# One pass over the in-projection's weights and one over the second half-step's, for all 576 tokens of a decoder step

## The chip, the cores and the metric

The kernel runs on one core of a Trainium2 chip. The metric is the device time of one execution in microseconds (us). In the profile PE is the matrix engine, DVE the vector engine, ACT the scalar engine, POOL the general engine and SP the engine that here only issues transfers. Each engine works through its own instructions in their order, and semaphores between them make one wait for another.

## The reference

One inference step of a two-layer decoder: 512 prompt tokens and 64 sample tokens (8 sequences of 8), 1024 features. Layer 0 is a half-step (SwiGLU), attention, a half-step; layer 1 is a half-step, a state space layer, a half-step. A layer norm stands behind each of the six.

```python
def ffn_residual(x, w_gate, w_up, w_down, g, b):
    return layer_norm(DN_ALPHA * x + FFN_RES * swiglu(x, w_gate, w_up, w_down), g, b)
for l in range(DEPTH):
    yp = ffn_residual(yp, ffn_w_gate[l, 0], ...); ys = ffn_residual(ys, ...)
    if l % 2 == 0:
        mp, ... = attn_mixer_prompt(yp, attn_w_in[i], attn_sinks[i], attn_w_out[i])
        ms, ... = attn_mixer_sample(ys, cache_a_k[i], cache_a_v[i], cache_b_k[i], cache_b_v[i], ...)
    else:
        ...  # state space layer
    yp = layer_norm(DN_ALPHA * yp + mp, ...); ys = layer_norm(DN_ALPHA * ys + ms, ...)
    yp = ffn_residual(yp, ffn_w_gate[l, 1], ...); ys = ffn_residual(ys, ...)
```

The attention has two mixers: A (8 heads, a mixture of three dilated windows over up to 2048 positions) and B (8 query heads over 2 key heads, the last 128 positions, with learned sinks). Prompt tokens attend within the prompt; sample tokens attend to 2048 cached keys and values per sequence and to their own.

## The kernel before, in words

Features lie on partitions, tokens are columns: `r` holds the residual, `xh` and `xl` the input of the next product as a pair (high and low part, float32r), so each product of a 128x128 block of weights is three matmuls (`product`). Columns come in two groups: GA (256, prompt) and GB (320: 64 sample tokens and 256 prompt tokens). `Weights` streams weights in units of at most 8 such blocks: SP loads a unit into a raw buffer (4 of them), ACT makes the high part (`hi`, L138), DVE the low part (`lo`, L145), into one of a few slots.

The order of the work is the order in which Python emits it. `hook()` runs after each product: it takes a step of what stands in `bg` (layer norms), else a step of each of the two tracks `lo[0]` and `lo[1]`, whose generators hold the attention in small steps. `lo_drain` steps the tracks until both are empty, with no product between.

- **Half-steps.** `ffn_joint` (layer 0, first) takes both groups per unit. `ffn_fast` (both of layer 1) does so too, and computes pairs of chunks of gate and up in seven block products instead of eight (`pair_run`). The second half-step of layer 0 is neither: `ffn_group` takes one group alone, so its weights are streamed twice, once for GA and once for GB, and there are no pairs.
- **In-projection.** Nine pairs of units, tiles of up to 128 tokens; a job (`in_job`) is 24 matmuls of 256 columns, `in_post` rotates queries and keys (`rope`: DVE, then POOL L1213) and later turns them (L1220). Group GA's 18 jobs come first, then 27 of GB with the weights streamed again.
- **Prompt attention.** 32 tasks, one for a pair of heads (A) or two heads (B) and a tile of 128 queries `p` = 0..3: scores (L1312), add bias and take the least value (DVE L1314), exponential (ACT L1321), scale (DVE L1325), three steps later transposes (L1337) and a copy (ACT L919), two steps later the product with the values (L1358, L1381) and `put_o` into `xh`, `xl`. The 16 tasks of p = 0, 1 run beside GB's projection, those of p = 2, 3 beside GA's half-step.
- **Samples.** `far_keys`: 48 steps, each of which issues the load of the next 128x512 tile `kc` of cached keys (ACT's queue, one ahead), multiplies a tile by the queries (DVE L1416) and adds it up (DVE L1417). `sample_b` is mixer B. `near` does one sequence's last 512 keys and values (2 MB each in two loads, 8 sequences); `far_values` streams 24 tiles `vc` of 512 KB (L1643). `near` starts only when `far_keys` is done (`first`).
- **Out-projection.** `end_group` for GA after the first 16 tasks, for GB (`out_b_now`) after all else of the attention, before the last part of GA's half-step; then follow the rest of GA's half-step and all of GB's (`ffn_b`).

So the emission order around the change is: 42 in-projection jobs; out-projection GA; 3 jobs; half-step GA without its last product, beside prompt attention, far keys and mixer B; near keys and far values in `lo_drain`; out-projection GB; end of half-step GA; half-step GB; layer 1.

## Time and profile before

| what | before |
|---|---|
| runs | 2422.57, 2427.65, 2423.44 us, median 2423.44 |
| profiled execution | span 2425.8 us from first to last instruction; its own time is not listed apart from the three runs |
| PE busy | 2313.1 us, 95% of the span |
| DVE, ACT, POOL busy | 1574.4, 946.3, 249.5 us |
| DMA | 307.04 MB, mean 127 GB/s |

Busy times say how long an engine had work in it, not how fast the work went. The granted clock (PEclk) is that of PE in tenths of full speed: 1.0 is 2.4 GHz, 0.5 is 1.2 GHz.

### The profile page before, as it was taken

The page shows a single profiled execution, that of the slowest core. Times are in us where ns is not written, and L with a number is a line of the kernel's source. Part 1 is how long each engine was busy: PE and PEld are TensorE (multiplying, and loading weights), DVE is VectorE, ACT ScalarE, POOL GpSimd, SP SyncE. Part 2 cuts the span into 40 slices and gives each one's busy share as a digit, 9 for nine tenths or more (in the row PEclk, how much of TensorE's full clock was granted, in tenths as well). Part 3 has the DMA queues.
Part 4 walks back from the last instruction along what each step waited for, and adds up shares of the span by engine and source line. Part 5 has one row for each costly group of instructions (what it writes and reads, how often), then busy time and mean ns, then how long its engine had stood idle before and what let it go on. Part 6 is the DMA issues. An engine that isn't in the chain of part 4 may idle for free.

```text
span 2425.8 us, 43680 instructions
## 1 busy us (share of the span) xinstructions
PE 2313.1 (95%) x17751; PEld 2241.5 (92%) x17751; DVE 1574.4 (65%) x3185; ACT 946.3 (39%) x1683; POOL 249.5 (10%) x388
## 2 busy tenths in 40 slices
PE   8999999999989988589999999999999999999998
PEld 8999999998878886379999999999999999999997
DVE  5878776766887765157544657667755565585675
ACT  3222232345476535135433433324346534342342
POOL 2012112131111000101100100000133101000000
PEclk9999999999999999689999999999999999999999
DMA  6244445354744798535655223423245312233241
GB/s 163 81 127 122 133 126 155 115 153 129 170 121 132 209 246 253 212 127 157 174 149 147 61 79 88 114 65 110 75 166 181 92 56 80 72 88 105 70 122 40
DMA packets 450858, 307.04 MB, mean 127 GB/s; under 512 B 13960, under 2 KB 420704, under 8 KB 450656
## 3 DMA queue, kind: packets, MB, share of 16 engines
q1 hardware_dynamic: 434944, 268.65, 38.0%
q0 software_dynamic: 7808, 20.38, 3.1%
q10 hardware_dynamic: 7904, 15.21, 2.2%
q8 instruction: 140, 2.29, 0.4%
q14 instruction: 62, 0.51, 0.1%
HBM read 282.07 MB, written 22.12 MB: 125 GB/s over the span
## 4 chain that ended last, share of the span: by engine, by line
PE 54%; DVE 8%; DMA 6%; ACT 4%; issue 2%; POOL 0%; SPq 0%; ACTq 0%; DVEq 0%; POOLq 0%
PE mm L588 11%; PE mm L587 11%; PE mm L589 11%; PE mm L736 4%; PE mm L738 4%; PE mm L737 4%; DMA kc<-in_cache_a_k_dram 2%; PE mm L580 2%; DMA vc<-in_cache_a_v_dram 2%; PE mm L582 2%; PE mm L584 2%; DVE wl L145 2%; ACT s L1321 1%; DMA wraw<-in_ffn_w_gate_dram 1%; DVE kc L1416 1%
## 5 line engine op out<-in xcount | busy, mean ns | idle before, releaser
L587 PE MATMUL mm<-xh,wh 128*128 128x320 f32 (+1 forms) x1880 | 562.8, 299 | 2.1 <-ACT xh L1664 1.2
L589 PE MATMUL mm<-xh,wl 128*128 128x320 f32 (+1 forms) x1880 | 558.9, 297 | 3.7 <-DVE wl L145 3.7
L588 PE MATMUL mm<-xl,wh 128*128 128x320 f32 (+1 forms) x1880 | 559.2, 297 | 0.1
L138 ACT CAST wh<-wraw 128x1024 fp32r<-128x1024 f32 (+2 forms) x440 | 437.0, 1001 | 303.0 <-PE mm L588 186.3
L145 DVE TENSOR_TENSOR wl<-wraw,wh 128x1024 fp32r<-128x1024 f32 (+2 forms) x440 | 508.2, 1165 | 39.7 <-ACT wh L138 39.4
L587 PE MATMUL mm<-hh,wh 128*128 128x320 f32 (+1 forms) x1408 | 421.7, 300 | 2.2 <-ACT hh L677 1.5
L589 PE MATMUL mm<-hh,wl 128*128 128x320 f32 (+1 forms) x1408 | 417.8, 297 | 5.2 <-DVE wl L145 5.2
L588 PE MATMUL mm<-hl,wh 128*128 128x320 f32 (+1 forms) x1408 | 417.4, 296 | 0.1
L589 PEld LDWEIGHTS mm<-xh,wl 128*128 128x128 f32 x1880 | 358.3, 191 | 4.9 <-DVE wl L145 4.9
L587 PEld LDWEIGHTS mm<-xh,wh 128*128 128x128 f32 x1880 | 358.6, 191 | 4.1 <-ACT xh L1664 1.6
L588 PEld LDWEIGHTS mm<-xl,wh 128*128 128x128 f32 x1880 | 358.5, 191 | 1.9 <-DVE xl L531 1.6
L589 PEld LDWEIGHTS mm<-hh,wl 128*128 128x128 f32 x1408 | 267.7, 190 | 6.0 <-DVE wl L145 6.0
L587 PEld LDWEIGHTS mm<-hh,wh 128*128 128x128 f32 x1408 | 267.8, 190 | 4.7 <-ACT hh L677 1.7
L588 PEld LDWEIGHTS mm<-hl,wh 128*128 128x128 f32 x1408 | 267.9, 190 | 0.8 <-DVE hl L679 0.3
L834 DVE TENSOR_TENSOR hf<-sg,mm 128x256 f32<-128x256 f32 (+1 forms) x128 | 57.8, 451 | 195.2 <-PE mm L589 96.3
L677 ACT CAST hh<-hf 128x256 fp32r<-128x256 f32 (+1 forms) x128 | 55.5, 433 | 307.4 <-DVE hf L834 307.4
L533 POOL TENSOR_SCALAR r<-r,lnb 128x256 f32<-128x256 f32 (+1 forms) x80 | 74.4, 947 | 867.3 <-DVE xl L531 867.3
L667 DVE TENSOR_TENSOR r<-r,mm 128x256 f32<-128x256 f32 (+1 forms) x96 | 43.3, 451 | 110.2 <-PE mm L589 110.2
L736 PE MATMUL mm<-sh,wh 128*128 128x288 f32 x384 | 113.5, 296 | 0.0
L737 PE MATMUL mm<-sl,wh 128*128 128x288 f32 x384 | 113.3, 295 | 0.0
L738 PE MATMUL mm<-sh,wl 128*128 128x288 f32 x384 | 113.0, 294 | 0.0
L1241 PE MATMUL mm<-wl,xh 128*128 128x256 f32 (+1 forms) x360 | 99.3, 288 | 8.8 <-DVE wl L145 8.8
(513 smaller groups left out, 4119.1 us busy)
## 6 DMA issues: line engine op xcount, KB each, us to landing
wraw<-in_ffn_w_gate_dram SPq DMA_DIRECT2D x110, 512.0 KB
wraw<-in_ffn_w_up_dram SPq DMA_DIRECT2D x110, 512.0 KB
wraw<-in_ffn_w_down_dram SPq DMA_DIRECT2D x80, 512.0 KB
wraw<-in_ffn_w_down_dram SPq DMA_DIRECT2D x40, 384.0 KB
wraw<-in_attn_w_in_dram SPq DMA_DIRECT2D x28, 512.0 KB
kc<-in_cache_a_k_dram ACTq DMA_DIRECT2D x48, 256.0 KB
vc<-in_cache_a_v_dram SPq DMA_DIRECT2D x24, 512.0 KB
kw<-in_cache_a_k_dram SPq DMA_DIRECT2D x16, 512.0 KB
```

The source lines that it names most:

```text
L138: self.nc.scalar.copy(u.h[:, :u.n], u.src)
L145: self.nc.vector.tensor_tensor(u.l[:, :u.n], u.src, u.h[:, :u.n].bitcast(F32), op=OP.subtract)
L533: nc.gpsimd.tensor_scalar(r[:, c, self.g], r[:, c, self.g], lnb[:, k:k + 1], self.scale, op0=OP.add, op1=OP.mult)
L587: nc.tensor.matmul(ps, u.h[:, ws(k)], th[:, k, g], start=k == 0, stop=False)
L588: nc.tensor.matmul(ps, u.h[:, ws(k)], tl[:, k, g], start=False, stop=False)
L589: nc.tensor.matmul(ps, u.l[:, ws(k)], th[:, k, g], start=False, stop=k == nk - 1)
L677: nc.scalar.copy(hh[:, c, t], hf)
L736: nc.tensor.matmul(ps, u.h[:, ws], xh_[:, k], start=k == 0, stop=False)
L737: nc.tensor.matmul(ps, u.h[:, ws], xl_[:, k], start=False, stop=False)
L738: nc.tensor.matmul(ps, u.l[:, ws], xh_[:, k], start=False, stop=k == 3)
L834: nc.vector.tensor_tensor(hf, sg, pu, op=OP.mult)
L1241: nc.tensor.matmul(ps, x, w, start=j == 0, stop=j == len(mms) - 1)
```

## The change

The in-projection takes all five tiles for each unit (the first three of nine pairs of units still in two sweeps, GA before GB, since GB's layer norm ends in between). All prompt attention and the far keys run beside the in-projection, and what is left of them in a `lo_drain` behind it. Since `xh`, `xl` are still the projection's input then, early outputs of the attention go to `r` (`put_o`), whose content is spilled to DRAM (`spill`, `fill`) and read back. Then come GA's out-projection with mixer B and the near keys on the tracks, a `lo_drain` for the rest of the samples, and GB's out-projection. The second half-step is one `ffn_fast` for both groups. The far keys' multiplications move from DVE to POOL, are loaded two ahead, and are added up one step later. `lo_drain` also pumps weights.

```diff
-P = {..., 'lr': 32, ...}
+P = {..., 'lr': 0, ...}
...
     def lo_drain():
         while any(t.busy() for t in lo):
             for t in lo:
                 t.step()
+            W.pump()
...
-            self.eps = eps4 if idx in (3, 5) else eps
-            self.scale = 1.0 if idx in (2, 4) else ALPHA
+            self.eps = eps4 if idx in (2, 3, 5) else eps
+            self.scale = 1.0 if idx in (1, 2, 4) else ALPHA
...
     def put_o(ps, c, t):
-        """a piece of the mixers' output, features on partitions, as the pair of the out projection"""
-        nc.scalar.copy(xh[:, c, t], ps)
-        nc.vector.tensor_tensor(xl[:, c, t], ps, xh[:, c, t].bitcast(F32), op=OP.subtract)
+        if o_waits[0]:
+            nc.scalar.copy(r[:, c, t], ps)
+            early_o.append((c, t))
+        else:
+            pair_o(ps, c, t)
...
-                    kc = kp.tile([128, 512], F32, name="kc")
+                    kc = kp.tile([128, 512], F32, name="kc", bufs=4)
                     q_far.dma_start(kc, far_rows(a["cache_a_k"], t, l, 1))
                     ks.append(kc)
+            def add_up(kc, l, t):
+                nc.vector.tensor_reduce(s_o[:, t, :, 0:2, l], kc.rearrange("p (j h d) -> p j h d", j=4, d=64), axis=AX.X, op=OP.add)
             load(0)
+            load(1)
             yield
+            last = None
             for i, (l, t) in enumerate(todo):
                 if t == 0:
                     q = qs.popleft()
-                load(i + 1)
+                load(i + 2)
                 kc = ks.popleft()
-                nc.vector.tensor_tensor(kc, kc, q, op=OP.mult)
-                nc.vector.tensor_reduce(s_o[:, t, :, 0:2, l], kc.rearrange("p (j h d) -> p j h d", j=4, d=64), axis=AX.X, op=OP.add)
+                nc.gpsimd.tensor_tensor(kc, kc, q, op=OP.mult)
+                if last:
+                    add_up(*last)
+                last = kc, l, t
                 yield
+            add_up(*last)
...
-        in_run(in_a, (0, 1), 2)
+        n0 = 3
+        jobs = [(ui, pair, i) for ui, pair in ins[:n0] for i in (0, 1)]
+        in_run(jobs, 2)
+        spill(GA)
         drain_bg()
-        lo[0].add([counted(g) for p in (0, 1) for g in prompt_tasks(prompt_a, p) + prompt_tasks(prompt_b, p)], P["pw"], P["pg"])
-        in_run(in_b[:P["fk"]], (2, 3, 4))
+        spill(GB_P)
+        o_waits[0] = True
+        W.slots(4)
+        in_run([(ui, pair, i) for ui, pair in ins[:n0] for i in (2, 3, 4)], 2)
         lo[1].add([far_keys()])
...
-        end_group(GA, out_a, xh, xl, NK, ev_add, 1, wait=P["wa"], spread=P["sa"])
-        in_run(in_b[P["nb"]:8], (2, 3, 4))
...
+        in_run(tile_jobs(n0, 4))
+        open_sm()
+        in_run(tile_jobs(4, 5))
+        lo[0].add(tasks(prompt_b, range(4)), P["pw"], P["pg"])
+        in_run(tile_jobs(5, 7))
+        lo[0].add(tasks(prompt_a, (0, 1)), P["pw"], P["pg"])
+        in_run(tile_jobs(7, 9))
+        in_flush()
+        o_waits[0] = False
+        lo[0].add(tasks(prompt_a, (2, 3)), P["pw"], P["pg"])
+        for g in (GA, GB_P):
+            for c in range(NK):
+                lo[1].add([from_r(c, g)], 2)
+            lo[1].add([fill(g)], 1, 1, True)
+        lo_drain()
...
+        mixer_b, near, far = sample_tasks(sa)
+        lo[1].add([mixer_b])
+        lo[0].add(near, P["sw"], P["sg"])
+        lo[0].add([far], 1, 1, True)
+        end_group(GA, out_a, xh, xl, NK, ev_add, 1, wait=P["wa"], spread=P["sa"])
+        drain_bg()
+        lo_drain()
+        st_s2.close()
+        st_s.close()
+        end_group(GB, out_b, xh, xl, NK, ev_add, 1, wait=1, spread=P["sb"])
...
-    attention(in_a, in_b, out_a, out_b, ffn_a)
+    attention(ins, out_a, out_b)
     W.slots(P["s8"])
-    ffn_group(ffn_b, GB, 2, wait=P["w0"])
+    ffn_fast(ffn01, 2, ahead=P["ah1"], wait=P["w1"], nslots=P["sn"], after=8)
     ffn_fast(ffn10, 3, ahead=P["ah1"], wait=P["w1"], nslots=P["sn"], after=4)
```

Three places show what moves. First, DVE beside GB's in-projection before the change: a far key step (L1416, L1417) stands between a rotation (L1202, L1207) and the next.

```order
L1149 TENSOR_TENSOR xl<-mm,xh 128x128
L1416 TENSOR_TENSOR kc<-kc,qb 128x512
L1417 TENSOR_REDUCE s_o<-kc 128x4x2
L1202 TENSOR_TENSOR sg<-mm,cos 128x256
L1207 TENSOR_TENSOR hf<-mm,sin 128x4x32 x2
```

In the changed kernel POOL has the multiplication (L1335), between the sum of a rotation (`rot`, L1123) and a copy of the sinks (L1285); DVE keeps the adding up (L1324 there). Behind the last rotation 24 multiplications follow each other on POOL, and then the reading back of `r` (L1602).

```order
L1123 TENSOR_TENSOR rot<-sg,hf 128x256
L1285 COPY s<-sink 128x2
L1335 TENSOR_TENSOR kc<-kc,qb 128x512
L1285 COPY s<-sink 128x2
L1335 TENSOR_TENSOR kc<-kc,qb 128x512 x24
L1602 DMA r<-d_r 128x8x256 x2
L1429 MEMSET blk_8509 128x128
```

So 48 multiplications leave DVE's row and stand in POOL's, 24 of them with nothing else around. Second, PE in the later half of the prompt attention, before: a product of GA's half-step (L580, L582, L584) stands between each task's pieces (values L1358, transposes L1337, scores L1312).

```order
L1312 MATMUL mm<-kT,qT_5547 128x512 x2
L580 MATMUL mm<-xh,wh_8490 128x256 x8
L582 MATMUL mm<-xh,wl_8491 128x256 x8
L584 MATMUL mm<-xl,wh_8490 128x256 x8
L1358 MATMUL mm<-pt,v 64x128 x6
L1337 MATMUL mm<-ident,s 128x128 x8
```

And in the changed kernel, behind the last job of the in-projection (values L1272, transposes L1251, scores L1226): twelve tasks more start behind it in this way, and no product is between them.

```order
L1272 MATMUL mm<-pt,v 64x128 x4
L1251 MATMUL mm<-ident,s 128x128 x6
L1226 MATMUL mm<-kT,qT_5564 128x128 x2
L1272 MATMUL mm<-pt,v 64x128 x6
L1251 MATMUL mm<-ident,s 128x128 x8
L1226 MATMUL mm<-kT,qT_5564 128x128 x2
```

Products have left this place. Third, PE where the near keys begin (transposes of `kw`). Before, they stand behind the last product of the half-step's part, and far key scores and the rest of the samples follow with no product.

```order
L589 MATMUL mm<-xh,wl_10945 128x256
L1526 MATMUL mm<-ident,kw 128x128 x16
L1517 MATMUL mm<-ident,s_o 128x128 x6
L1542 MATMUL mm<-kt,blk_9484 32x512 x4
L1545 MATMUL mm<-k_s,blk_9484 32x8 x4
L1526 MATMUL mm<-ident,kw 128x128 x16
```

In the changed kernel the first of them stands behind the first product of GA's out-projection, and the second product follows.

```order
L549 MATMUL mm<-xh,wh_7646 128x256
L550 MATMUL mm<-xl,wh_7646 128x256
L551 MATMUL mm<-xh,wl_7647 128x256
L1447 MATMUL mm<-ident,kw 128x128 x16
L549 MATMUL mm<-xh,wh_7649 128x256
L550 MATMUL mm<-xl,wh_7649 128x256
```

So seven of the eight products of GA's out-projection now stand among the first steps of the samples.

## Rows read from the trace of the kernel before

**Rows 1.** The page: busy times in us (share of the span), instructions.
```profile
PE 2313.1 (95%) x17751; PEld 2241.5 (92%) x17751; DVE 1574.4 (65%) x3185; ACT 946.3 (39%) x1683; POOL 249.5 (10%) x388
```
**Rows 2.** Stretches: us, busy PE, PEld, DVE, ACT, POOL, PEclk, DMA share, GB/s.
```profile
469.00:640.60 171.60, 161.45 (x1293) 147.21 (x1291) 121.24 (x310) 78.55 (x189) 44.83 (x60) 0.97 0.51 149
640.60:668.40 27.80, 24.75 (x197) 23.73 (x195) 24.00 (x42) 11.92 (x17) 1.48 (x2) 1.00 0.90 190
668.40:681.70 13.30, 11.30 (x93) 10.67 (x92) 13.20 (x28) 4.66 (x11) 1.80 (x2) 1.00 0.73 185
681.70:927.50 245.80, 225.64 (x1794) 206.85 (x1795) 176.21 (x350) 139.38 (x248) 14.53 (x33) 0.98 0.66 179
927.50:989.60 62.10, 51.81 (x575) 35.45 (x573) 28.61 (x102) 32.91 (x71) 7.09 (x26) 0.92 0.78 253
989.60:1047.90 58.30, 27.02 (x393) 16.59 (x392) 2.67 (x7) 1.00 (x3) 4.51 (x9) 0.50 0.47 190
1047.90:1078.40 30.50, 30.47 (x195) 30.14 (x196) 19.75 (x30) 12.51 (x17) 0.00 (x0) 0.94 0.37 109
1078.40:1345.20 266.80, 261.80 (x1810) 260.66 (x1810) 161.12 (x225) 116.92 (x167) 20.92 (x16) 0.99 0.53 155
1345.20:1751.60 406.40, 406.40 (x3047) 405.82 (x3047) 264.35 (x461) 144.67 (x245) 14.64 (x16) 1.00 0.29 82
```
**Rows 3.** The same view: jobs with tasks, five steady jobs, steady products of 256 columns.
```profile
526.00:640.00 114.00, 111.41 (x921) 98.69 (x920) 78.82 (x239) 54.90 (x149) 19.59 (x30) 1.00 0.50 143
513.80:529.40 15.60, 15.60 (x132) 15.51 (x131) 8.94 (x20) 6.01 (x11) 6.16 (x6) 1.00 0.71 206
1352.00:1369.40 17.40, 17.40 (x147) 17.40 (x146) 14.58 (x27) 7.26 (x15) 8.62 (x8) 1.00 0.11 32
```
**Rows 4.** The same, of single lines on PE: mixer B's first (L1438) and last (L1484).
```profile
682.00:927.00 245.00, 1.28 (x8) 0.91 (x8) 0.98 0.66 179
...
682.00:927.00 245.00, 1.12 (x2) 0.29 (x2) 0.98 0.66 179
```
**Rows 5.** Groups on DVE, 469 to 526: busy us, mean ns, idle before, releaser.
```profile
L524 DVE SCALAR_TENSOR_TENSOR r<-r,lng,lnaccB 128x320 f32<-128x320 f32 x8 | 5.7, 752 | 0.1
L531 DVE SCALAR_TENSOR_TENSOR xl<-r,lnb,xh 128x320 fp32r<-128x320 f32 x8 | 4.7, 609 | 0.7 <-ACT xh L525 0.7
L445 DVE TENSOR_TENSOR r<-r,lnsB 128x640 f32<-128x640 f32 x4 | 3.3, 817 | 0.0
L531 DVE SCALAR_TENSOR_TENSOR xl<-r,lnb,xh 128x256 fp32r<-128x256 f32 x3 | 1.9, 696 | 0.0
```
**Rows 6.** Groups on DVE and ACT, 683 to 790, prompt attention beside GA's half-step.
```profile
L1417 DVE TENSOR_REDUCE s_o<-kc 128x8 f32<-128x512 f32 x10 | 6.9, 689 | 0.3
L1314 DVE CUSTOM_DVE_ANT_0 s<-mm,bias_a 128x512 f32<-128x512 f32 x8 | 5.2, 684 | 0.0
L1149 DVE TENSOR_TENSOR xl<-mm,xh 128x128 fp32r<-128x128 f32 x16 | 4.5, 284 | 0.6 <-ACT xh L1148 0.5
L1325 DVE TENSOR_SCALAR s<-s,den 128x512 f32<-128x512 f32 x8 | 3.5, 484 | 0.1
L531 DVE SCALAR_TENSOR_TENSOR xl<-r,lnb,xh 128x256 fp32r<-128x256 f32 x8 | 3.2, 467 | 0.0
L1322 DVE RECIPROCAL den<-den 128x2 f32<-128x2 f32 x16 | 2.7, 166 | 18.8 <-ACT s L1321 18.8
L1321 ACT ACT_TABLE_LOAD x7 | 9.0, 1283 | 1.6 <-DVE st L1314 1.5
```
**Rows 7.** Groups on POOL, 460 to 1110.
```profile
L1213 POOL TENSOR_TENSOR rot<-sg,hf 128x256 f32<-128x256 f32 x24 | 22.8, 951 | 65.8 <-DVE hf L1207 51.7 <-issue 7.4 <-DVE xl L1149 3.6
L1601 POOL TENSOR_TENSOR pb<-pof,mask 128x512 f32<-128x512 f32 x6 | 6.4, 1067 | 47.6 <-PE aux L1643 32.1 <-ACT pof L1619 15.5
```
**Rows 8.** Far keys in the chain, 600 to 690 (start, us): shortest and longest landing.
```profile
622.93 4.41 DMA kc<-in_cache_a_k_dram
628.80 7.01 DMA kc<-in_cache_a_k_dram
```

More of the change, by code (lines that the diff above doesn't have):

```diff
@@ L27 @@
 SMP = slice(256, 320)
+GB_P = slice(320, TOK)
 HALF = 320
@@ L1287, in in_post, with in_run @@
                 q_out.dma_start(d_q[:, cs], rot)
-        def in_run(units, tiles, fresh=0):
-            for m, (ui, pair) in enumerate(units):
-                for i in tiles:
-                    ps = in_job(pair, i, m < fresh)
-                    while len(pend) > 1:
-                        pend.popleft()()
-                    W.pump()
-                    in_post(ui, i, ps)
-                    hook()
+        def in_run(jobs, fresh=0):
+            for m, (ui, pair, i) in enumerate(jobs):
+                ps = in_job(pair, i, m < fresh)
+                while len(pend) > 1:
+                    pend.popleft()()
+                W.pump()
+                in_post(ui, i, ps)
+                hook()
         def in_flush():
@@ L1680, in sample_tasks @@
-            return [sample_b(sa)], [first()], [near(b) for b in range(8)], [far_values()]
-        def samples(*sts):
-            for st in sts:
-                st.close()
-            sa = st_s2.enter_context(tc.tile_pool(name="sa", bufs=2, reuse_waits="tile"))
-            b, l, n, f = sample_tasks(sa)
-            lo[0].add(b)
-            lo[0].add(l, 1, 1, True)
-            lo[0].add(n, P["sw"], P["sg"], True)
-            lo[0].add(f, 1, 1, True)
+            pn = sa.tile([128, 64], F32, name="pn", bufs=1)
@@ new lines, in sample_tasks, with spill @@
+            acc = sa.tile([128, 4, 64], F32, name="acc", bufs=1)
+            for n, x, xs in (("cache_a_k", "kw", kws), ("cache_a_v", "vw", vws)):
+                xs[0] = load_near(n, 0, x)
+            mixer_b = sample_b(sa)
+            next(mixer_b)
+            for n, x, xs in (("cache_a_k", "kw", kws), ("cache_a_v", "vw", vws)):
+                xs[1] = load_near(n, 1, x)
+            return mixer_b, [near(b) for b in range(8)], far_values()
+        def spill(g):
+            nc.gpsimd.dma_start(d_r[:, :, g], r[:, :, g])
@@ new lines, in tile_jobs, with tasks @@
+        def tile_jobs(x, y):
+            return [(ui, pair, i) for ui, pair in ins[x:y] for i in (2, 0, 1, 3, 4)]
+        def tasks(f, js):
+            return [f(j, p) for p in range(4) for j in js]
+        in_run(tile_jobs(n0, 4))
[6 more added lines that the diff above has]
+        in_flush()
@@ new lines, in attention @@
+        o_waits[0] = False
[5 more added lines that the diff above has]
+        lo_drain()
+        for st in (st_m, st_f, st_k, st_p):
+            st.close()
+        sa = st_s2.enter_context(tc.tile_pool(name="sa", bufs=2, reuse_waits="tile"))
+        mixer_b, near, far = sample_tasks(sa)
+        lo[1].add([mixer_b])
+        lo[0].add(near, P["sw"], P["sg"])
@@ L1713, in attention @@
+        lo[0].add([far], 1, 1, True)
         end_group(GA, out_a, xh, xl, NK, ev_add, 1, wait=P["wa"], spread=P["sa"])
-        in_run(in_b[P["nb"]:8], (2, 3, 4))
-        lo[0].add([g for f in (prompt_a, prompt_b) for p in (2, 3) for g in prompt_tasks(f, p)], P["pw2"], P["pg2"], batch=P["pb2"])
-        in_run(in_b[8:], (2, 3, 4))
         drain_bg()
-        for _ in range(P["fl"]):
-            lo[0].step()
-        rate[1] = P["r1c"]
-        def flush():
-            in_flush()
-            st_k.close()
-            return
-            yield
```

241 lines of the change are left out of this document (54 added, 187 removed).

## The prediction, made before the changed kernel ran

> **What bounds the kernel now.** I read the page first: PE is busy for 95% of the span [rows 1]. A busy PE can be a waiting one, so next come the stretches. From 469 us (first job of the in-projection) to 1345.2 us (first product of layer 1) pass 876.2 us, and this is the part that the change rewrites. The reader is to see two kinds of stretch there [rows 2]. In layer 1's first half-step (1345.2 to 1751.6) PE is never idle. In the samples' stretch (927.5 to 1047.9, 120.4 us) nothing covers the near keys and the far values: PE is busy for 51.81 of 62.1 us, then for 27.02 of 58.3 us at a granted clock of 0.50, which is 1.2 GHz, after the preceding stretch at 0.92 with gaps.
>
> I split the 876.2 us by work. Steady products of 256 columns come every 17.40 / 147 = 0.1184 us, and a job of the in-projection takes 15.60 / 5 = 3.12 us with its turns [rows 3]. In 681.7 to 927.5 GA's half-step has 44 x 24 matmuls of gate and up and 8 x 3 x (6 + 8) of down, 1392 in all: 164.8 us. Mixer B has 10.1 us on PE, summed over seven lines [rows 4]. The rest of this stretch, 245.8 - 164.8 - 10.1 = 70.9 us, is the later prompt attention with its waits. So, from [rows 2]:
>
> - second half-step: 164.8 + 266.8 = 431.6 us;
> - in-projection with prompt attention: 171.6 + 13.3 + 70.9 = 255.8 us;
> - GA's out-projection, mixer B, samples: 27.8 + 10.1 + 62.1 + 58.3 = 158.3 us;
> - GB's out-projection: 30.5 us.
>
> **The second half-step** becomes the program of layer 1's first one, for the same tokens and sizes. That one takes 406.4 us [rows 2], so 431.6 - 406.4 = 25.2 us go. Most of it is arithmetic: six pairs of chunks, for gate and up, spare one block product of 12 matmuls per seven and pair and group of two halves, 12 x 12 = 144 matmuls of 406.4 / 3047 = 0.133 us, 19.2 us. The rest are the waits of two separate runs. The halved streaming of weights and the halved splitting on ACT and DVE I cost at nothing: where PE runs with no idle time, they are hidden already. Its start needs eight units within GA's first 8 products of 24 x 0.1184 = 2.84 us, as layer 1's does; if they came late, some 3 to 6 us.
>
> **In-projection with prompt attention.** The matmuls are the same 45 jobs; what changes is the cover.
> - The first 15 jobs: 15 x 3.12 = 46.8 us. Only six jobs of GA now stand before GB's, not 18, and GB's layer norm has 5.7 + 4.7 + 3.3 = 13.7 us of work on DVE [rows 5], of which about one job, 3.1 us, stays hidden: 10.6 us of wait (0 if it starts earlier, 13.7 if nothing hides it). 57.4 us.
> - Ten jobs with far keys alone: 31.2 us and some 2 for the first landing. 33 us.
> - Twenty jobs with twenty tasks: 62.4 us, and per task what it adds now. In 526 to 640 24 jobs and 16 tasks took 114.0 us [rows 3], a task (114.0 - 24 x 3.12) / 16 = 2.45 us. That holds some waits of DVE for far keys, which POOL now takes two loads ahead. 62.4 + 49 = 111 as an upper bound, 100 with the waits gone; I take 105.
> - The tail. Twelve tasks start behind the last job, in a drain of 18 far key steps, and no product covers them. A round of the widest task has on DVE 2 x 0.684 (scores), 0.166, 2 x 0.484 (scaling), 0.284 and 0.689 (adding up), 3.48 us, and each task made DVE wait 18.8 / 16 = 1.18 us for the exponentials [rows 6]: 4.65 us. The twelve have a mean width of 363 of 512 columns; if the 2.34 us that depend on width shrink by as much, it is 3.97. 12 x 4.3 = 52 us, and six rounds of about 2 us that only end tasks and far keys, 12: 64 us. PE's work is less than that, and the old cover for it, GA's half-step, is gone; with DVE's waits overlapped it could be 45.
>
> Together 57.4 + 33 + 105 + 64 = 259.4 us, 3.6 more than before. The attention no longer alternates with the half-step's Silu; 7 of the loads of ACT's table, 1.283 us each, stood before exponentials in 107 us [rows 6], and as many before Silu. ACT was busy there for 139.38 of 245.8 us [rows 2], so I give this no term of its own: it is part of why the tail's rounds are not priced as the old ones.
>
> **Out-projection GA, mixer B, samples.** The samples' own 62.1 + 58.3 us stay, since nothing new covers far values. Now GA's products, 192 x 0.1184 = 22.7 us, and mixer B, 10.1, stand among the near keys. PE was already busy for 51.81 of 62.1 us there, so I hide none of it. I add 8 us: GA's layer norm has no cover behind it (0 to 11 us, 13.7 x 256 / 320), and the first two sequences' 4 MB, which came early before, are fetched here. 161.2 us, 2.9 more than before. The spilling of `r` I cost at nothing at its start (the DMA share was 0.51 [rows 2]); its return belongs to this stretch's bytes, below.
>
> **Sum.** 406.4 + 259.4 + 161.2 + 30.5 = 857.5 us for 876.2, a gain of 18.7 us, on a span of 2425.8 us that lies 2.4 above the median of the three runs. From the median: 2423.4 - 18.7 = 2405 us.
>
> **A price that the trace does not show.** POOL never multiplied two such tiles. Its nearest rows are a sum of 256 columns at 0.951 us and a product of 512 at 1.067 us [rows 7]; for 512 columns of two tiles I bound it by 1.07 and 1.9 and take 1.5. With a rotation it stays under a job's 3.12 us, so POOL is not the bound. Beside POOL's work DVE is slower at times: the low part of 256 columns took 0.696 us where POOL worked on `r`, and 0.467 later [rows 5, 6].
>
> **The rivals.**
> - *Far keys set the pace (slower).* With no product in a round, 18 rounds may each wait for a load. Landings that held up the chain took 4.41 to 7.01 us [rows 8], mid 5.7: 18 x 5.7 = 103 instead of 64 us, 2444 us. It decides from (64 + 18.7) / 18 = 4.6 us per round. Against it: loads now run two ahead, and ACT's issue is not behind a wait for them.
> - *POOL and DVE shut each other out (slower).* If each of the tail's multiplications held up DVE's scalings, 18 x 1.07 to 1.9 us, 19 to 34 us, would join the tail: 2424 to 2439 us. It decides from 1.04 us a round. For it speaks the 0.696 against 0.467 us; against it, that a round's scores and adding up read one SBUF tile or PSUM. The Trainium skill, page "SBUF — State Buffer", section "Who interferes with whom", says that DVE in a two-port mode, or with two SBUF inputs, and a POOL instruction that reads SBUF exclude each other for a whole instruction; by that rule moving the multiplications is no free gain. This trace agrees in direction (0.696 us), but shows no such pair for the far keys.
> - *The samples' bytes set the pace (slower).* 253 GB/s x 62.1 us are 15.7 MB; now come 4 MB of first sequences, 1 of mixer B, 2.1 of `r` and 4.2 of weights, 27 MB. At 253 GB/s 107 us, near my 103; at the far values' 190 GB/s 142 us: 2444 us.
> - *The tail overlaps well (faster).* Tail 45, jobs 100, samples 150: 19 + 5 + 11 us less, 2370 us.
> - *The covers lost eat the gain:* the terms in between, 2419 to 2428 us.
>
> **Chances.** My forecast (2392 to 2418) 0.45, good overlap 0.20, no change 0.12, far keys' pace 0.10, samples' bytes 0.08, POOL and DVE 0.05. Under 0.2%, 4.8 us, a measurement of this kernel cannot tell from no change: faster 0.65, same 0.12, slower 0.23. The range is 2372 to 2444 us, which leaves out about one in ten on each side.
>
> **What would show it.** The second half-step in some 406 us with PE busy throughout; a stretch of about 64 us behind the last job with no product; near keys and far values of about 160 us with GA's out-projection among the first; the far values again at clock 0.50. I am wrong in the tail if DVE or POOL there waits for `kc` in most rounds, and in the samples if near keys wait for `kw` beyond the first two.

## The result: 1.4% slower, where 0.8% faster was forecast

The changed kernel takes 2459.09 us (median of four runs, 2451.65 to 2470.49), the kernel before 2425.55 on the same chips. The ratio is 1.014, 95% interval 1.0112 to 1.0169. The time lies outside the range of the prediction (2372 to 2444) and on the other side of no change.

The page of the profile hides it. Its line of busy times, for [rows 1]:

```profile
PE 2305.5 (94%) x17629; PEld 2230.6 (91%) x17629; DVE 1550.4 (63%) x3242; ACT 874.7 (36%) x1642; POOL 299.3 (12%) x440
```

PE has less work than before, and so have DVE and ACT. The stretches of the changed kernel, for [rows 2] (us, busy PE, PEld, DVE, ACT, POOL, PEclk, DMA share, GB/s; from start to start of a piece of work on PE), show where the time went:

```profile
468.10:537.10 69.00, 54.24 (x405) 51.81 (x403) 34.93 (x80) 15.12 (x34) 27.58 (x36) 0.88 0.28 85
537.10:568.10 31.00, 31.00 (x260) 30.55 (x259) 16.97 (x41) 7.19 (x15) 19.14 (x20) 1.00 0.62 172
568.10:660.80 92.70, 91.33 (x734) 78.28 (x734) 60.09 (x194) 46.32 (x136) 39.16 (x49) 0.98 0.48 139
660.80:722.60 61.80, 51.57 (x311) 31.98 (x311) 43.77 (x127) 33.92 (x101) 18.11 (x14) 0.81 0.35 108
...
722.60:856.70 134.10, 89.52 (x851) 70.50 (x851) 71.06 (x193) 55.80 (x116) 24.69 (x56) 0.82 0.61 194
856.70:923.70 67.00, 26.48 (x393) 15.87 (x392) 2.67 (x7) 0.99 (x2) 5.52 (x10) 0.53 0.47 172
923.70:955.07 31.37, 31.33 (x194) 31.00 (x195) 17.45 (x28) 11.58 (x16) 0.00 (x0) 0.91 0.25 72
955.07:1372.10 417.03, 409.63 (x3064) 409.04 (x3063) 270.99 (x467) 150.74 (x252) 12.10 (x16) 0.99 0.31 88
1372.10:1787.06 414.96, 411.41 (x3064) 410.50 (x3063) 268.32 (x469) 146.83 (x249) 12.10 (x16) 0.99 0.29 82
1787.06:2458.20 671.14, 647.41 (x4914) 641.86 (x4912) 417.61 (x726) 269.49 (x489) 68.74 (x103) 0.98 0.32 99
```

Beside the terms of the prediction, in us:

| term | predicted | measured | difference |
|---|---|---|---|
| first 15 jobs | 57.4 | 69.0 | +11.6 |
| ten jobs, far keys | 33 | 31.0 | -2.0 |
| twenty jobs, twenty tasks | 105 | 92.7 | -12.3 |
| drain (the tail) | 64 | 61.8 | -2.2 |
| out-projection GA, mixer B, near keys | 102.9 | 134.1 | +31.2 |
| far values | 58.3 | 67.0 | +8.7 |
| out-projection GB | 30.5 | 31.4 | +0.9 |
| second half-step | 406.4 | 417.0 | +10.6 |
| next half-step (layer 1's first) | 406.4, not in the sum | 415.0 | +8.6 |
| the rest and the start | 674.2 and 469.0 | 671.1 and 468.1 | -4.0 |

The differences add up to 51.1 us, which is what lies between the forecast change of the span (-18.7) and the measured one (2458.2 - 2425.8 = +32.4). In-projection and prompt attention are right in sum, 254.5 for 259.4. Two terms fail: the samples' stretch, and the half-steps, where 431.6 + 406.4 = 838.0 us before became 417.0 + 415.0 = 832.0: of 25.2 us, 6 are left.

**Inside the samples' stretch.** The groups of waits on PE from 722 to 857 us (who waits, for what: us in total, times, longest) begin so:

```profile
PE mm L1438 <- DVE r L629: 12.9, 1, 12.9
PE mm L1502 <- DMA vw<-in_cache_a_v_dram: 7.2, 4, 5.2
PE mm L1447 <- DVE xl L1415: 5.9, 1, 5.9
PE mm L1447 <- DVE sst L1472: 3.4, 1, 3.4
```

The first is the longest stop. DVE's L629 adds a product of GA's out-projection to `r`, and `r` is not back yet: DVE itself waits 7.0 us for the load `r<-d_r`, of which GA's part lands 8.8 us after its issue and GB's 10.9. POOL issues GA's part behind the far keys' last multiplication. The chain of work that ended last shows from 716 us on why that is so late (start, us, what; DMA rows are loads under way, "x4" four instructions of a kind):

```profile
716.12 8.23 DMA kc<-in_cache_a_k_dram
...
724.48 1.31 POOL kc L1335
...
726.53 9.29 DMA kc<-in_cache_a_k_dram
...
735.96 1.27 POOL kc L1335
...
737.25 0.69 DVE s_o L1324
...
737.93 1.21 DVE xl L1064 x4
...
739.43 0.06 POOL r L1602
```

The last far key loads take 8.2 and 9.3 us. By the time the last of them is issued, SP has issued 2 MB of the samples (four loads of 512 KB, from 713.5 to 724.4 us), and from 716 to 736 us the packets of SP's queue took 45% of the DMA engines' time, those of the far keys' queue 30%. (Two expectations below speak of 8 MB of first loads; the first two sequences are 4 MB and mixer B 1 MB.) Behind each load stand POOL's multiplication and DVE's adding up. GA's part of `r`, the one that L629 needs, is issued at 737.15, right behind POOL's last multiplication; GB's part also waits for the low parts (L1064).

POOL's own waits, first from 716 to 747 us, then from 660.8 (the end of the last job) to 738, show that the prediction's tail is not over when PE leaves it at 722.6:

```profile
POOL kc L1335 <- DMA kc<-in_cache_a_k_dram: 14.7, 6, 7.1
```

```profile
POOL kc L1335 <- DMA kc<-in_cache_a_k_dram: 40.1, 15, 7.1
```

The last six multiplications take 22.4 us, from 714.8 to 737.2, where the prediction has six rounds of about 2 us. The far keys end 76.4 us after the last job, not 64. And 15 of the 19 multiplications behind the last job wait for `kc`: that is the sign by which the prediction wanted to be found wrong in its tail.

The rows of POOL's timeline 40 us later show the second stop: LN's eight updates of `r` stand ahead of the copy that the near keys' softmax waits for.

```profile
796.88 6.14 POOL L535 TENSOR_SCALAR r<-r,lnb 128x256 f32<-128x256 f32 x8 [45.77 <-issue]
802.98 0.26 POOL L1468 COPY srow<-so 128x96 f32<-128x96 f32 x1
```

Mixer B's last copies (L1415) follow, the third row above. While near keys wait, no new near load is issued either: from 800 to 815 us the DMA moved 11 GB/s.

**At the entries of the half-steps**, by stretches (columns as above), the second half-step first, then the next one:

```profile
955.07:963.00 7.93, 7.79 (x64) 7.42 (x62) 6.83 (x9) 3.77 (x5) 0.00 (x0) 1.00 0.78 227
963.00:970.30 7.30, 0.05 (x1) 0.08 (x1) 2.49 (x5) 5.36 (x8) 0.00 (x0) 0.75 0.90 238
970.30:980.00 9.70, 9.70 (x69) 9.70 (x70) 7.99 (x15) 4.79 (x9) 2.83 (x4) 0.83 0.19 56
```

```profile
1372.10:1380.00 7.90, 4.35 (x36) 4.09 (x34) 7.69 (x14) 5.25 (x8) 0.00 (x0) 0.98 0.58 172
1380.00:1390.00 10.00, 10.00 (x58) 9.61 (x59) 6.79 (x13) 4.15 (x9) 0.00 (x0) 0.67 0.34 100
```

PE stands for 7.3 us in the one and 3.4 us in the other, and pays twice: behind each stop the granted clock is below 1.0 for some 10 us (0.83 from 970.3, 0.67 from 1380). In [rows 2] the next half-step has neither. Both stops are waits for GB's layer norm:

```profile
PE aux L459 <- DVE lnst L497: 7.4, 1, 7.4
PE aux L452 <- DVE lnsB L441: 3.4, 1, 3.4
```

ACT's timeline ahead of the first shows what holds the norm (in brackets the idle time before and what ended it):

```profile
962.64 1.04 ACT L139 CAST wh<-wraw 128x1024 fp32r<-128x1024 f32 x1 [2.17 <-DMA wraw<-in_ffn_w_gate_dram]
965.17 1.04 ACT L139 CAST wh<-wraw 128x1024 fp32r<-128x1024 f32 x1 [1.49 <-DMA wraw<-in_ffn_w_up_dram]
...
967.81 0.17 ACT L492 ACTIVATE lnst<-aux 128x3 f32<-128x3 f32 x1
```

The norm's step L492 stands behind casts of weights that have only just landed.

### The profile page after: what moved, and what is told of

It is laid out like the page before. It is cut to its first block, busy times and chain, and to the rows that moved or that the text cites. A ratio compares the mean times of both kernels' runs of the same rounds, so it can differ in the third digit from the quotient of the medians.

```text
span 2458.2 us, 43285 instructions
## 1 busy us (share of the span) xinstructions
PE 2305.5 (94%) x17629; PEld 2230.6 (91%) x17629; DVE 1550.4 (63%) x3242; ACT 874.7 (36%) x1642; POOL 299.3 (12%) x440
## 4 chain that ended last, share of the span: by engine, by line
PE 81%; DVE 7%; DMA 5%; issue 3%; ACT 2%; POOL 1%; SPq 0%; ACTq 0%; DVEq 0%; POOLq 0%
PE mm L549 16%; PE mm L550 16%; PE mm L551 15%; PE mm L698 5%; PE mm L700 5%; PE mm L699 5%; PE mm L1151 5%; DMA vc<-in_cache_a_v_dram 2%; PE mm L542 2%; PE mm L544 2%; PE mm L546 2%; DVE r L415 1%; DVE wl L146 1%; DMA kc<-in_cache_a_k_dram 1%; DMA vw<-in_cache_a_v_dram 1%
## 5 line engine op out<-in xcount | busy, mean ns | idle before, releaser
L549 PE MATMUL mm<-xh,wh 128*128 128x320 f32 (+1 forms) x1560 | 468.8, 301 | 2.2 <-ACT xh L1585 1.2
L550 PE MATMUL mm<-xl,wh 128*128 128x320 f32 (+1 forms) x1560 | 465.1, 298 | 0.5 <-DVE xl L533 0.5
L551 PE MATMUL mm<-xh,wl 128*128 128x320 f32 (+1 forms) x1560 | 464.7, 298 | 0.0
L139 ACT CAST wh<-wraw 128x1024 fp32r<-128x1024 f32 (+2 forms) x366 | 357.4, 983 | 265.2 <-PE mm L550 200.7
L146 DVE TENSOR_TENSOR wl<-wraw,wh 128x1024 fp32r<-128x1024 f32 (+2 forms) x366 | 415.5, 1143 | 48.0 <-ACT wh L139 48.0
L549 PEld LDWEIGHTS mm<-xh,wh 128*128 128x128 f32 x1560 | 298.8, 192 | 3.1 <-ACT xh L1585 1.6
L550 PEld LDWEIGHTS mm<-xl,wh 128*128 128x128 f32 x1560 | 298.8, 192 | 1.1 <-DVE xl L533 0.7
L551 PEld LDWEIGHTS mm<-xh,wl 128*128 128x128 f32 x1560 | 298.5, 191 | 0.0
L629 DVE TENSOR_TENSOR r<-r,mm 128x320 f32<-128x320 f32 (+1 forms) x128 | 57.8, 452 | 159.5 <-PE mm L551 152.4
L698 PE MATMUL mm<-xh,wh 128*128 128x288 f32 x432 | 127.2, 294 | 0.0
```

Of the source, the lines that this page charges most:

```text
L139: self.nc.scalar.copy(u.h[:, :u.n], u.src)
L146: self.nc.vector.tensor_tensor(u.l[:, :u.n], u.src, u.h[:, :u.n].bitcast(F32), op=OP.subtract)
L549: nc.tensor.matmul(ps, u.h[:, ws(k)], th[:, k, g], start=k == 0, stop=False)
L550: nc.tensor.matmul(ps, u.h[:, ws(k)], tl[:, k, g], start=False, stop=False)
L551: nc.tensor.matmul(ps, u.l[:, ws(k)], th[:, k, g], start=False, stop=k == nk - 1)
L629: nc.vector.tensor_tensor(r[:, c, g], r[:, c, g], ps, op=OP.add)
```

## Experiments

Twelve kernels ran. The first nine change one thing in the changed kernel, but for the fifth, which changes two; the last three combine what helped. In the tables and texts "the stretch" is that from GA's out-projection to far values (134.1 us above). Of five kernels with the same code there (the changed one, and the runs named two passes, slots early, two products and far keys on DVE) it took 133.1 to 137.7 us, and their far values 56.9 to 76.6. What a gain in the stretch costs ahead of it shows in the sum of jobs, drain and stretch: 192.7 + 61.8 + 134.1 = 388.6 us in the changed kernel, 386.9 to 394.2 in the three runs with the same code all the way (two passes, slots early, two products), 362.3 in the prediction.

**Two passes of the second half-step.**
```diff
-P = {..., 'lr': 0, ...}
+P = {..., 'lr': 32, ...}
...
-    ffn_fast(ffn01, 2, ...)
+    ffn_group(ffn_a, GA, 2)
+    ffn_group(ffn_b, GB, 2, wait=P["w0"])
```


> The changed kernel with its second half-step undone: GA alone, then GB alone, weights streamed twice, no pairs, as before the change. In the changed kernel this half-step took 417.0 us and the next one 415.0, before 431.6 and 406.4 (prediction: 406.4 for each). Theory F (the single pass loses covers: a layer norm that GA's or GB's products hid now stands bare at the entry of each of the two half-steps, 10.6 and 8.7 us): the two return to about 431.6 and 406, in all 838 for 832, and the kernel is 4 to 8 us slower than the changed one. Rival (the single pass is worth its 25 us, and the 8.7 us of the next half-step have another cause, such as bytes or weights that come late): the next half-step stays at 415, and the kernel is 12 to 17 us slower than the changed one.

Measured: 2467.05 us, ratio to the kernel before 1.0187 (1.0164 to 1.0211), some 11 us more than the changed kernel (4 to 8 were expected). The two half-steps:

```profile
953.80:1389.20 435.40, 428.44 (x3202) 427.90 (x3201) 253.80 (x345) 194.31 (x273) 18.64 (x16) 0.99 0.57 165
1389.20:1795.70 406.50, 406.50 (x3049) 405.92 (x3048) 264.75 (x462) 144.39 (x244) 16.22 (x16) 1.00 0.29 82
```

The next half-step is back at 406.5 us with no stop, so its 8.6 us belong to the single pass (theory F), or to the form of GB's norm, `lr`, which the edit restores with it; no run parts the two. The stop at the start of the second half-step stays (PE waits 7.0 us for GB's norm): that one does not come from the single pass, and there theory F is wrong. The pass is worth 841.9 - 832.0 = 9.9 us, not 25.

**1.7 far key steps per product.**
```diff
         lo[1].add([far_keys()])
+        rate[1] = 1.7
...
         o_waits[0] = False
+        rate[1] = 1
```


> The changed kernel with 1.7 far key steps per product beside the in-projection, not 1, so that none of the 48 is left for the drain. Theory S (order: in the samples' stretch of 201.1 us engines wait behind instructions that stand late; the first piece are 13.0 us in which the accumulation of GA's out-projection waits for the return of r, issued on POOL behind the last multiplication, which ended at 737.2): the gap goes, the last far key steps at 717 to 738 go, and from the last job to GB's out-projection 261.2 us become 238 to 248; the kernel is 12 to 22 us faster than the changed one, 2437 to 2447. Rival B (bytes: the loads of the samples, r and the weights set the pace, 185 to 206 GB/s on average): the bytes of the far keys leave the drain, but the gap only moves to the next wait for a load; 255 to 262 us, and the jobs beside which the far keys now run grow by what is saved.

Measured: 2451.7 us, ratio 1.014 (1.0096 to 1.0184), no gain in total (12 to 22 us were expected). The stretch is 120.0 us, the drain 47.9, both as theory S says; but the jobs take 217.5 us for 192.7, and the sum is 385.4. The stretch shrinks though nearly all of its bytes are left in it, and the far keys cost elsewhere what they save here.

**r read back on the other track.**
```diff
-                lo[1].add([from_r(c, g)], 2)
-            lo[1].add([fill(g)], 1, 1, True)
+        lo[0].add([from_r(c, g) for g in (GA, GB_P) for c in range(NK)], 30, 1, False, 16)
+        lo[0].add([fill(g) for g in (GA, GB_P)], 30, 1, False, 2)
```


> The changed kernel with the reading back of r and the copies ahead of it moved from the far keys' track to that of the prompt tasks, so that POOL issues it ahead of the last six multiplications. Theory S: the accumulation no longer waits at 733.6, PE waits at most for the last far key sums (737.9 us, where now 746.6), and the stretch of the samples is 6 to 10 us shorter; the kernel is 5 to 10 us faster than the changed one. Rival B (bytes): the same loads land at the same time in another order, the stretch stays within 3 us of 201.1.

Measured: 2448.2 us, ratio 1.0119 (1.01 to 1.0139). The stretch is 129.0 us, 5.1 less, where 6 to 10 were expected. The wait for `r` shrinks as expected, from 12.9 to 4.9 us, and another takes part of its place:

```profile
PE mm L1447 <- DMA kw<-in_cache_a_k_dram: 6.8, 1, 6.8
PE mm L1447 <- DVE xl L1415: 6.5, 1, 6.5
PE mm L1438 <- DVE r L629: 4.9, 1, 4.9
```

**GA's out-projection ahead of the samples.**
```diff
-        lo[1].add([mixer_b])
-        lo[0].add(near, P["sw"], P["sg"])
-        lo[0].add([far], 1, 1, True)
         end_group(GA, out_a, ...)
         drain_bg()
+        lo[1].add([mixer_b])
+        lo[0].add(near, P["sw"], P["sg"])
+        lo[0].add([far], 1, 1, True)
```


> The changed kernel with GA's out-projection and its layer norm ahead of the samples, nothing of the samples beside them. Theory S: out-projection 22.7 us and some 13 of wait for r, 10 of layer norm, then mixer B and near keys as before the change, about 62 + 12, and far values 58 to 66: 178 to 186 us in place of 201.1, the kernel 15 to 23 us faster than the changed one. Rival C (the products beside the samples hide work, and what is slow is slow for other reasons): the 22.7 us of products are no longer hidden, and the stretch grows to 210 to 224 us.

Measured: 2444.57 us, ratio 1.0122 (1.0074 to 1.0171). 44.2 + 81.7 + 58.5 = 184.4 us for 201.1, in the band of theory S, of which 8.5 in the far values prove nothing. Up to far values that is 125.9 us for 134.1, so taking the products away from the samples costs nothing in sum: what they hid there was no more than the stops that came with them.

**Mixer B alone beside the out-projection** (with `r` read back on the other track; near keys behind the norm).
```diff
         lo[1].add([mixer_b])
-        lo[0].add(near, P["sw"], P["sg"])
-        lo[0].add([far], 1, 1, True)
         end_group(GA, out_a, ...)
         drain_bg()
+        lo[0].add(near, P["sw"], P["sg"])
+        lo[0].add([far], 1, 1, True)
```


> The changed kernel with the reading back of r on the prompt tasks' track (as in the run before that moved it) and only mixer B beside GA's out-projection; near keys start when its layer norm is done. The best run so far took 184.4 us from GA's out-projection to GB's (44.2 of it for the out-projection with its norm alone, 81.7 for mixer B and near keys, 58.5 for far values). Theory S (order): mixer B, 10 us of matmuls and its small steps, runs in the waits of the out-projection, which now waits less for r; 33 to 40 + 62 to 68 + 59 = 155 to 167 us, as before the change (158.3), and the kernel takes 2418 to 2432 us. Rival B (bytes): the near keys' loads set the pace, 80 us for near keys whatever stands beside them; 175 to 185 us, 2438 to 2448.

Measured: 2439.14 us, ratio 1.0052 (1.0035 to 1.0069). 61.2 + 64.7 + 61.2 = 187.1 us. The near keys take 64.7 us, close to the 62.1 before the change and not rival B's 80; but the out-projection takes 61.2 us for 33 to 40, and so the total misses theory S's band (2418 to 2432) and falls in rival B's (2438 to 2448). The out-projection's longest wait is for a load of mixer B:

```profile
PE mm L1360 <- DMA bk<-in_cache_b_k_dram: 14.5, 1, 14.5
```

**Slots for weights opened earlier.**
```diff
+        W.slots(P["s8"])
         end_group(GB, out_b, ...)
```


> The changed kernel with the eight slots for weights opened ahead of GB's out-projection, not behind it, so that the second half-step's first units can be cast and split during it. In the changed kernel this half-step begins with 7.3 us in which PE waits for GB's layer norm, whose steps on ACT stand behind casts of units that had just landed (238 GB/s there). Theory W (late weights): the wait shrinks to 0 to 2 us, the half-step takes 407 to 410 us and not 417.0, if GB's out-projection grows by no more than 2. Rival N (the norm's own chain on DVE and ACT behind one product of cover): the wait stays at 6 to 8 us.

Measured: 2444.46 us, ratio 1.0077 (1.0043 to 1.0111). The second half-step:

```profile
962.70:1370.70 408.00, 408.00 (x3065) 407.58 (x3064) 266.27 (x463) 146.72 (x248) 12.09 (x16) 1.00 0.30 84
```

PE is never idle in it, and GB's out-projection did not grow (29.1 us). Theory W holds: 9 of the 10.6 us were weights that came late, whose casts held GB's norm. The next half-step keeps its stop (414.4 us).

**Two products of cover for GB's norms.**
```diff
-        end_group(GB, out_b, xh, xl, NK, ev_add, 1, wait=1, ...)
+        end_group(GB, out_b, xh, xl, NK, ev_add, 1, wait=2, ...)
...
-    ffn_fast(ffn01, 2, ahead=P["ah1"], wait=P["w1"], ...)
+    ffn_fast(ffn01, 2, ahead=P["ah1"], wait=2, ...)
```


> The changed kernel with GB's layer norm given two products of cover, not one, before PE takes its sums, ahead of the second half-step and ahead of the next one. Theory N (a norm that is not ready holds PE, and with PE its clock): at the next half-step the wait of 3.4 us goes and the stretch behind it is no longer at a clock of 0.67, so 406 to 408 us in place of 415.0; at the second half-step the same, 408 to 411 in place of 417.0, if the weights are there. Rival W (late weights or bytes): PE waits as long for a weight one product later; 416 and 414.

Measured: 2447.53 us, ratio 1.0087 (1.007 to 1.0103).

```profile
951.00:1366.60 415.60, 410.60 (x3065) 410.00 (x3064) 270.47 (x467) 150.99 (x252) 11.82 (x16) 0.99 0.31 88
1366.60:1777.10 410.50, 409.84 (x3064) 408.92 (x3064) 267.14 (x469) 146.72 (x249) 13.52 (x16) 1.00 0.29 83
```

The two entries differ, as they should if the causes differ: the next half-step loses 4.5 us, a little less than theory N says (a wait of 0.6 us is left, and 10 us at a clock of 0.83); the second one loses 1.4 (PE still waits 5.0 us for the norm), as rival W says: its weights are still late.

**Far keys' multiplications on DVE again.**
```diff
-                nc.gpsimd.tensor_tensor(kc, kc, q, op=OP.mult)
+                nc.vector.tensor_tensor(kc, kc, q, op=OP.mult)
```


> The changed kernel with the far keys' 48 multiplications on DVE again (0.686 us each before the change) and not on POOL (1.27 us there); loads stay two ahead. If POOL's work held up DVE in the drain (the rival of the prediction), the drain's rounds of 3.3 us shrink or stay, 55 to 60 us, although DVE has 0.69 more in each. If the move was a gain, the drain grows by 19 x 0.69 = 13 us to 73, the twenty jobs with tasks by 21 x 0.4 to 0.69 = 8 to 14, and the kernel is 10 to 25 us slower than the changed one; the return of r, behind 24 multiplications on POOL no more, gives 5 to 8 of that back.

Measured: 2456.69 us, ratio 1.0147 (1.0104 to 1.019), the same as the changed kernel, so neither expectation came true (a drain of 55 to 60, or of 73 and a kernel 10 to 25 us slower). Drain 62.5 us for 61.8, stretch 135.1 for 134.1. No multiplication stands ahead of the return of `r` on POOL now, and its GA part is issued at 705.8 us; yet PE waits for the accumulation all the same, for about half as long, and the stretch is no shorter:

```profile
PE mm L1438 <- DVE r L629: 6.0, 1, 6.0
```

DVE's L629 stands behind DVE's own multiplications, and these wait for the same late loads of far keys (9.9 us from 720 to 770). So it is the far keys' last loads that hold up the start of the stretch, on whichever engine.

In the drain DVE has 11.0 us of multiplications more, and the drain is only 0.7 us longer. One part of the answer is in DVE's scaling of the probabilities (L1239), first in the drain of the changed kernel, then here (count, shortest, median and longest in ns):

```profile
L1239 DVE TENSOR_SCALAR s<-s,den x26: 274/448/1215, 664.2 to 715.0; 128x384 f32<-128x384 f32 x8, 128x512 f32<-128x512 f32 x8, 128x256 f32<-128x256 f32 x6, 128x128 f32<-128x128 f32 x4
```

```profile
L1239 DVE TENSOR_SCALAR s<-s,den x26: 280/418/488, 668.5 to 721.5; 128x384 f32<-128x384 f32 x8, 128x512 f32<-128x512 f32 x8, 128x256 f32<-128x256 f32 x6, 128x128 f32<-128x128 f32 x4
```

With the multiplications on POOL (1.27 us each) the longest scaling takes 1.215 us, with them on DVE 0.488; in sum 13.6 against 9.4 us. The longest is one of 128x128, which takes 0.28 us otherwise; in the changed kernel it starts just behind a multiplication and ends just behind it (two scalings in DVE's row):

```profile
688.71 1.27 POOL L1335 TENSOR_TENSOR kc<-kc,qb 128x512 f32<-128x512 f32 x1 [2.62 <-DMA kc<-in_cache_a_k_dram]
688.85 1.41 DVE L1239 TENSOR_SCALAR s<-s,den 128x128 f32<-128x128 f32 x2
```

The other part, not tested by itself, is that DVE waits 11.4 us for exponentials in either drain, so that a multiplication of 0.68 us can find room. The Trainium skill, page "SBUF — State Buffer", section "Who interferes with whom", says that DVE in a two-port mode and POOL lock each other out for a whole instruction; the trace agrees: a scaling is at times longer by most of a multiplication. It costs 4 us here, not the 19 to 34 of the rival, as 7 of the 26 scalings are caught.

**1.4 far key steps beside the twenty jobs with tasks.**
```diff
         lo[0].add(tasks(prompt_b, range(4)), P["pw"], P["pg"])
+        rate[1] = 1.4
...
         o_waits[0] = False
+        rate[1] = 1
```


> The changed kernel with 1.4 far key steps per product beside the twenty jobs with tasks (1 beside the ten before them, as now), so that about 10 of 48 are left for the drain, not 18, and the last is loaded before the samples' first 8 MB are. Theory S in its narrower form (the last far key loads, which took 8.2 and 9.3 us behind the near keys' loads, hold POOL, with POOL the return of r, and with DVE's adding up the accumulation of GA's out-projection): the 13.0 us gap goes to 5 or less, the stretch from GA's out-projection to far values shrinks from 134.1 (133 to 138 in the runs with the same code there) to 118 to 126, the drain from 61.8 to 54 to 60, and the jobs grow by 0 to 5 us, not by 24.8 as with 1.7 steps; the kernel is 10 to 20 us faster than the changed one, 2438 to 2450. Rival B (bytes): the stretch stays at 130 to 138, since the same 8 MB must land.

Measured: 2445.13 us, ratio 1.0098 (1.0083 to 1.0113). Stretch 122.2 us (the wait for `r` is gone), drain 59.7, both in the bands; but the jobs take 204.1 us for 192.7, where 0 to 5 more were expected, and the sum is 386.0 for 388.6: what the stretch saves, the jobs pay. Most of this run's gain over the changed kernel lies in far values (56.6 us for 67.0), which the edit does not touch. POOL waits 17.9 us for `kc` in the jobs with tasks where it waited 8.6; the rotations stand behind that. From the program's order: a far key step that comes twice in a job finds its load not landed, as it is issued two steps ahead and not a fixed time ahead.

**The combination** of 1.4 steps, `r` read back on the other track, mixer B alone beside the out-projection with its loads first, slots earlier and two products of cover (the edits above, and in `sample_tasks`):
```diff
+            mixer_b = sample_b(sa)
+            next(mixer_b)
             for n, x, xs in (("cache_a_k", "kw", kws), ...):
                 xs[0] = load_near(n, 0, x)
-            mixer_b = sample_b(sa)
-            next(mixer_b)
```


> All that helped, together: far keys at 1.4 steps, r read back on the prompt tasks' track, mixer B alone beside GA's out-projection and its own loads ahead of the near keys', near keys behind it, slots for weights opened ahead of GB's out-projection, and two products of cover for GB's norms. If the stalls are separate, as theory S, W and N say: jobs 193 to 196, drain 55 to 60, out-projection with mixer B 35 to 45, near keys 62 to 66, far values 57 to 67, out-projection GB 29 to 31, half-steps 407 to 410 and 409 to 412, the rest as before: 2392 to 2415 us, 0.5 to 1.3% faster than the kernel before. Rival B (bytes): the samples' 27 MB take 185 us in any order, and only the half-steps gain: 2425 to 2435.

Measured: 2425.29 us, ratio 1.0025 (1.0004 to 1.0046), above theory S's band (2392 to 2415) and at the edge of rival B's (2425 to 2435).

```profile
470.10:677.10 207.00, 180.05 (x1395) 163.60 (x1395) 119.29 (x321) 67.51 (x185) 98.23 (x114) 0.93 0.44 126
677.10:735.70 58.60, 48.42 (x311) 30.17 (x311) 43.17 (x132) 34.73 (x105) 19.15 (x19) 0.83 0.39 112
735.70:776.80 41.10, 33.49 (x259) 31.41 (x259) 28.99 (x59) 17.03 (x27) 2.41 (x10) 0.91 0.68 221
776.80:845.80 69.00, 57.30 (x596) 42.00 (x598) 36.79 (x125) 37.54 (x85) 13.61 (x36) 0.85 0.68 223
...
935.80:1343.70 407.90, 407.90 (x3064) 407.48 (x3063) 265.79 (x463) 146.83 (x248) 11.82 (x16) 1.00 0.30 84
1343.70:1754.20 410.50, 409.83 (x3065) 409.15 (x3064) 267.28 (x469) 146.83 (x249) 13.52 (x16) 1.00 0.29 83
```

The stalls are separate: the stretch is 41.1 + 69.0 = 110.1 us for 134.1, and the half-steps 818.4 for 832.0. The jobs give 14.3 us of it back (207.0), so that the sum is 375.7. Rival B's total comes out, its reason does not: the samples take 110.1 + 59.2 = 169.3 us, not 185.

**The samples' first loads behind the far keys'** (the combination with one far key step per product; mixer B's loads and the near keys' and values' first 4 MB on ACT's queue):
```diff
-        rate[1] = 1.4
...
+                q = q_far if b < 2 else q_near
-                    q_near.dma_start(x[h], ...)
+                    q.dma_start(x[h], ...)
```


> The combination of the last run with two things other: the far keys at one step per product again, and the samples' first loads (mixer B's 1 MB and the near keys' and values' first 8 MB) issued on ACT's queue, behind the far keys' loads, not on SP's, where they overtook them. Theory S (the far keys' last loads were overtaken): jobs back to 191 to 196 (207.0 in the combination), no load of a far key over 6 us, out-projection with mixer B 35 to 45 (41.1), near keys 62 to 70 (69.0): 2405 to 2418 us. Rival B (bytes): what is loaded later is waited for later, near keys grow by the 10 to 14 us that the jobs give back; 2420 to 2430.

Measured: 2426.13 us, ratio 1.002 (0.9992 to 1.0048). The total is in rival B's band (2420 to 2430). The jobs are back at 192.0, as expected, near keys take 66.1, and the sum is 369.6, the least of all runs; but the out-projection with mixer B takes 52.8 us, with 8.5 of wait for `bk`, and POOL still waited 8.6 us for one far key load, while the 2 MB of `r` were under way. That the samples' loads had overtaken the far keys' is thus not the whole cause of late far keys: here the loads of `r` took their place. Far values took 70.3 us in this run. Here rival B is right in part: in these 15 us the DMA moved 276 GB/s, and a load put behind another is waited for instead of it.

**The same, near keys among the norm's steps.**
```diff
-        drain_bg()
         lo[0].add(near, P["sw"], P["sg"])
         lo[0].add([far], 1, 1, True)
+        while bg:
+            step_bg()
+            for t in lo:
+                t.step()
```


> As the run beside it, but the near keys begin with the steps of GA's layer norm and not behind it. Theory: the norm of GA's out-projection (10 to 16 us from its last product to the first near key in the combination) gets cover from the near keys' transposes and scores, 4 to 8 us less from out-projection to far values; 2400 to 2414. Rival (as in the changed kernel, norm and near keys get in each other's way on DVE, ACT and POOL): 0 to 10 us more than the run beside it.

Measured: 2424.42 us, ratio 0.9994 (0.9984 to 1.0005), no different from the kernel before. The stretch is 124.2 us for 118.9 beside it, as the rival says; in the profiled executions its total is no worse, since its far values took 59.5 us and the other's 70.3. No version here beats the kernel before.

## Why the prediction was wrong

**The half-steps.** "Becomes the program of layer 1's first one ... takes 406.4" took the time of a program out of its surroundings. The program is the same; its entry is not. Before the change the last part of GA's half-step ran between GB's out-projection and any use of GB's norm, and GB's half-step hid GA's norm. Now the second half-step starts right behind GB's out-projection, its weights come mostly then (DMA moved 72 GB/s during the out-projection, 227 and 238 behind it), and their casts hold GB's norm: shown by the earlier slots, 417.0 to 408.0. At the next entry both norms end together: shown by the two passes (415.0 to 406.5, with the norm's form restored too) and in half by the second product of cover (to 410.5). The prediction named late weights at "some 3 to 6 us" and priced them at nothing; they cost 9. The next half-step's entry was in no term. A stop also costs the clock behind it (10.6 us were lost around a stop of 7.3, 8.6 around one of 3.4), which the sum never had.

**The samples' stretch** was the term furthest off: 161.2 predicted, 201.1 measured. Its "I add 8 us" stands where 201.1 - 62.1 - 58.3 - 22.7 - 10.1 = 47.9 were. Of the 31.2 us up to far values, 11.9 go from the stretch with the far keys' last loads and the return of `r` (134.1 to 122.2 with 1.4 steps), 12.1 more in the combination (to 110.1), which also undoes the tangle of norm, mixer B and near keys; 7.2 are left. But the 1.4 steps only move their share into the jobs. What is won shows in the sum of jobs, drain and stretch: 388.6 us, some 10 less with `r` on the other track and mixer B alone beside the out-projection (378.3), some 9 less again with mixer B's loads first and the samples' first loads behind the far keys' (369.6), which leaves 7 over the prediction's 362.3. How these gains divide among the single edits was not tried, and runs with the same code differ by 7. The order of POOL, printed ahead of the prediction, had a part of the cause in three rows: 24 multiplications, then the return of `r`. It was cost as bytes ("its return belongs to this stretch's bytes"), not as a place in a queue. With the multiplications on DVE the stretch stays at 135.1 us, so the late loads ahead of them count for more than the engine. The rival on the samples' bytes named the place but not the mechanism: DMA idles at 11 GB/s for 15 us in the midst of it, and the stretch shrinks with the same bytes. In the last two runs, with the stops gone, bytes do begin to count.

**Far values**, 67.0 for 58.3, are not explained by the change: runs with the same code gave 56.9 to 76.6 us.

**In-projection and prompt attention** came out right (254.5 for 259.4), by two errors that cancel: the first 15 jobs took 69.0 for 57.4, since one stop for a rotation on POOL (7.5 us) and GB's norm (7.3 us in waits for `xh`) come with a clock of 0.88, and the twenty tasks 92.7 for 105. The drain's 61.8 for 64 is in part luck too. Its rounds with scores were sized rightly (52 predicted, and 54.0 us pass from the last job to 714.8), but the last six far key steps, priced at 12, took 22.4, and PE left for the out-projection before they ended. The rival "far keys set the pace" did not come true in PE's time there, but its mechanism, late loads of `kc`, is what the prediction's argument against it ("loads now run two ahead") had wrong, and it decided the start of the stretch behind.

**POOL for DVE** was priced at 1.07 to 1.9 us, and took 1.27; it neither gained nor lost anything that total times show.

## What to carry to other kernels

When two loops over the weights become one, ask at each of its ends which layer norm, load or cast the second loop used to hide, and bill each stop a second time for the clock that follows it. When a step moves to another engine, read that engine's order to the end: what stands behind the last moved instruction (here the return of `r`) inherits its waits. Judge a gain in one stretch by its sum with the stretches that feed it. And a time taken from a twin elsewhere in the kernel holds for its middle, not for its entry.

## What the runs showed of the hardware

Far values read 12 MB by the same loads at two speeds with the same share of busy DMA engines. The first 20 us of them in the run with earlier slots, then in that with two products of cover:

```profile
856.00:876.00 20.00, 5.65 (x104) 4.47 (x104) 1.25 (x5) 0.39 (x4) 3.20 (x6) 0.63 0.52 131
```

```profile
863.00:883.00 20.00, 10.39 (x163) 6.93 (x162) 0.84 (x2) 0.00 (x0) 2.74 (x6) 0.50 0.52 210
```

131 and 210 GB/s at a share of 0.52; in the first run the speed rose to about 210 after some 45 us. Both ran on the same chip. The cause was not found. Differences of up to 20 us between two runs in this stretch are therefore no evidence on an edit.
